# Square sums cast on ScalarE, their columns added by matmuls with ones, and a loader one deeper, in a two-block sequence model on Trainium2

## The chip, the cores and the metric

The kernel runs on one core of one Trainium2 chip. The metric is the device time of one execution in microseconds; several executions of the same kernel are timed and the median is taken. A profile of one execution gives, for every instruction on TensorE (PE, with its weight loads as PEld), VectorE (DVE), ScalarE (ACT), GpSimd (POOL) and SyncE (SP), its start, its duration and what ended the idle time before it.

## The reference, cut to what matters

Two blocks are chained, each on 2048 rows of width 1024, all in float32:

```python
def first_block(x, ...):
    xn = rmsnorm(x, norm_gain)
    proj = xn @ w_in                            # 1024 x 3072
    u, z, h, b, c, zc = pieces of proj, 512 wide each
    y_ssm  = s5_mixer(u, ..., w_glu, b_glu) * silu(z)
             # state-space scan, gelu, then y * sigmoid(y @ w_glu + b_glu)
    y_conv = b * conv3(c * h) * silu(zc)
    return rmsnorm(x + concat(y_ssm, y_conv) @ w_out, final_norm_gain)

def second_block(x, c, ...):
    sh1, sc1, g1, sh2, sc2, g2 = split(silu(c) @ w_ada + b_ada, 6)
    p = (x * (1 + sc1) + sh1) @ w_in_2
    y = concat(conv_module(...),                # 31 taps, layer norm, silu
               hgrn2_mixer(...),                # gated recurrence, 4 heads
               chunk_attention(...)) @ w_out_2  # chunks of 64, 8 chunks back
    x = layer_norm(ALPHA * x + (1 + g1) * y)
    gt, up = split((x * (1 + sc2) + sh2) @ w_ffn_in, 2)    # 2816 each
    return layer_norm(ALPHA * x + (1 + g2) * ((silu(gt) * up) @ w_ffn_out))

reference(x, ...) = second_block(first_block(x, ...), c_2, ...)
```

## The kernel before

Every large product is computed in fp16 with three passes: each float32 operand is scaled by a power of two and split into a high and a low half, and `mm3` (L417, L418, L419) adds high x high, high x low and low x high in one PSUM bank of 128 x 512.

The scale comes from the sum of the operand's squares. The steps, which are those that the change touches, are the same wherever an operand is made ready:

1. `sumsq` (L410): ScalarE squares the tile and leaves one sum for each partition (an ACTIVATE, then an ACTIVATION_READ_ACCUMULATOR of one column). A tile in several pieces has a column for each piece.
2. `part`: VectorE turns the column into bf16 (L365), or adds two columns and writes bf16 (L367). A weight with two or four columns is first added up by a VectorE reduce (L186).
3. `total` (L373): one TensorE matmul with a 128 x 128 matrix of ones adds the column over the partitions and gives every partition the sum. VectorE makes the scale and its inverse out of it (`pow2`, L354 to L356; where the sum itself is kept, a copy to `tot` stands ahead of it).
4. `split`: ScalarE writes the high half (L405), VectorE the low half (L406).

There are 82 such totals. They come from `Weight` (a weight of 128 columns has one column of sums, one of 256 has two, one of 512 has four), `Pair` (an FFN weight, in two pieces: `scale` is the Square and `part`, `cut` the total and the splits), `gp1`/`gp2` and `mp1`/`mp2` (the operands of the GLU and of the first block's out-projection; `mp1` has two columns), and `project` of the FFN, whose column is a VectorE reduce.

A `Loader` takes a list of weights through load (a DMA on SyncE's queue, L169), Square and `part` (`stat`), and total and split (`split`). Each `step` does at most one of each. `d1` is how many loads ahead a Square waits for, `d2` how many loads ahead a split waits for; a weight that is loaded but not split holds its raw float32 tile, 4 KB per partition for 128 columns. `Loader.run` is a generator that other stages advance tick by tick. It passes over a tick when the arena, the pool that all buffers come from, has no room.

The stage around the change of depth is the end of the first block, `stage_glu_mix`. For 16 row blocks t of 128 rows and for each of two halves n of 512 columns it multiplies by `w_out` (24 matmuls), adds the result to x on VectorE (L1079), and calls `k.bg.tick()`, which advances what runs in the background; then come the squares and scale of the final norm, and the tail of the row block before (norm gain, shift, split, the store of x at L1050, two transposing DMAs at L1060). From row block 8 on the background includes `ConvAtt.prep`, whose loader brings in nine weights of the second block's first projections: W0 to W7 with 128 columns, W8 with 256. W0's total stands on TensorE ahead of the second half of row block 9 and W8's ahead of the second half of row block 13. After the sixteen row blocks come the second block's projections from these weights (`proj`).

Each engine runs its instructions in the order in which a scheduler has put them, by its own simulated times, before the program is built. A matmul behind a total in TensorE's order waits with it. `k.several`, `k.pair`, `k.new` and `k.tiny` take buffers from the arena or from a ring of small columns; `k.hold` takes columns that are kept.

Of the kernel before, what the change touches and what calls it, by code (L numbers as in the profile page):

```python
# [11 lines left out]
BF16 = mybir.dt.bfloat16  # L12
# [3 lines left out]
ALU = mybir.AluOpType  # L16
AX = mybir.AxisListType
# [135 lines left out]
class Weight:  # L153
# [17 lines left out]
    def stat(self):  # L171
        k = self.k
        nc = k.nc
        n = len(self.raw)
        self.pair = k.pair([P, self.nkb, self.ncol], "w")
        ss = k.tiny("wss", n)
        for c, raw in enumerate(self.raw):
            if self.colmul is not None:
                cm = self.colmul[:, c * P:(c + 1) * P].unsqueeze(1).to_broadcast([P, self.nkb, P])
                k.gtt(raw, raw, cm, ALU.mult)  # L180
            if self.rowmul is not None:
                self.mul(raw, raw, self.rowmul.unsqueeze(2).to_broadcast([P, self.nkb, P]), ALU.mult)
            k.sumsq(self.pair[1][:, :, c * P:(c + 1) * P].bitcast(BF16), raw, out=ss[:, c:c + 1])
        if n > 1:
            t = k.tiny("wst")
            nc.vector.tensor_reduce(t, ss, axis=AX.X, op=ALU.add)  # L186
            ss = t
        self.cols = k.cols3.pop(0) if len(k.cols3) > 8 else k.hold(3)
        self.tot, self.s, self.inv = (self.cols[:, i:i + 1] for i in range(3))
        self.x = k.part(self.tot, ss)  # L190

    def split(self):
        k = self.k
# [15 lines left out]
class Loader:  # L209
# [6 lines left out]
    def step(self):  # L216
        n, total = self.n, len(self.ws)
        if n[0] < total and n[0] <= n[2] + self.d2:
            self.ws[n[0]].load()
            n[0] += 1  # L220
        if n[1] < n[0] and (n[1] + self.d1 < n[0] or n[0] == total):
            self.ws[n[1]].stat()
            n[1] += 1
        if n[2] < n[1] and (n[2] + self.d2 < n[0] or n[1] == total):
            self.ws[n[2]].split()
            n[2] += 1
        return n[2] < total
# [43 lines left out]
class Kit:  # L271
# [87 lines left out]
    def gtt(self, out, x, y, op):  # L359
        self.nc.gpsimd.tensor_tensor(out, x, y, op)  # L360

    def part(self, col, a, b=None):
        x = col.bitcast(BF16)[:, :1]
        if b is None:
            self.nc.vector.tensor_copy(x, a)  # L365
        else:
            self.nc.vector.tensor_tensor(x, a, b, ALU.add)  # L367
        return x

    def total(self, x, out, tot=None):  # L370
        nc = self.nc
        ps = self.bank()
        nc.tensor.matmul(ps[:, :1], self.ones, x, start=True, stop=True)  # L373
        sq = ps[:, :1]
        if tot is not None:
            nc.vector.tensor_copy(tot, sq)
            sq = tot
        self.pow2(sq, out=out)
        self.unbank(ps)
# [543 lines left out]
def stage_glu_mix(k, a, xT, chunks, ssm, mod, dr, nxt):  # L923
    nc = k.nc
# [49 lines left out]
    def mp1(tb):  # L974
        cv = k.new([P, 4, TB], F32, "cv")
        nc.sync.dma_start(cv, dr["yv"][:, tb * TB:(tb + 1) * TB].rearrange("(k p) t -> p k t", p=P))
        gy = G[tb][0]
        pr = k.pair([P, KB, TB], "mp")
        s2 = k.tiny("ms", 2)
        k.sumsq(pr[1][:, 0:4].bitcast(BF16), gy, out=s2[:, 0:1])  # L980
        k.sumsq(pr[1][:, 4:8].bitcast(BF16), cv, out=s2[:, 1:2])
        s, inv = k.hold(), k.hold()
        k.part(inv, s2[:, 0:1], s2[:, 1:2])
        M[tb] = [gy, cv, pr, s, inv]

    def mp2(tb):
        gy, cv, pr, s, inv = M[tb]
        k.total(inv.bitcast(BF16)[:, :1], (s, inv))
        k.split(pr[0][:, 0:4], pr[1][:, 0:4], gy, s)
        k.split(pr[0][:, 4:8], pr[1][:, 4:8], cv, s)  # L990
        k.free(gy, cv)
        sc = k.hold(2)
        for n in range(2):
            v.tensor_tensor(sc[:, n:n + 1], inv, wo[n].get(0).inv, ALU.mult)
        M[tb] = (pr, sc)

    wl = k.bg.add(wloads(), 1.0)
    for f in range(4):
        w = chunks.get(16 + f, 1)
        for tb in range(NTB):  # L1000
            ps = k.fm(w, xT[tb])
# [19 lines left out]
    gp2(2)  # L1021
    gp1(3)
    mp2(0)
    mp1(1)
    md = dr["mod"][0]
# [6 lines left out]
    g(2)  # L1032
    gp2(3)
    mp2(1)
    xs = {}
    hTs = {}
# [32 lines left out]
    for tb in range(NTB):  # L1069
        pr, sc = M[tb]  # L1070
        for i in range(4):
            t = tb * 4 + i
            if t + 2 < 16:
                load(t + 2)
            x = xs[t]
            for n in range(2):
                ps = k.tm(wo[n].get(0), pr, i)
                xsl = x[:, n * 512:(n + 1) * 512]
                v.scalar_tensor_tensor(xsl, ps, sc[:, n:n + 1], xsl, op0=ALU.mult, op1=ALU.add)  # L1079
                k.unbank(ps)  # L1080
                k.bg.tick()
            junk = k.new([P, D], BF16, "junk")
            ss = k.sumsq(junk, x)
            k.free(junk)
            xs[t] = (x, k.rsqrt(ss, 1.0 / D, 1e-6))
            if t >= 1:
                tail(t - 1)
            if i == 1 and tb + 2 < NTB:
                mp1(tb + 2)
            if i == 3 and tb + 2 < NTB:  # L1090
                mp2(tb + 2)
        k.free(*pr)
        if tb == 0:
            g(3)
        if tb < 3:
            nxt(tb, inv_h, hb2)
# [28 lines left out]
def att_bias(k, a, ext_d, scl):  # L1125
    nc = k.nc
    B = [k.new([P, 640], F32, "B") for _ in range(4)]
    for h in range(4):
        ex = k.new([P, 768], F32, "ex")
        nc.sync.dma_start(ex[:, 511:767], a["rel_bias_2"][0, h, 0:256].partition_broadcast(P))  # L1130
        nc.gpsimd.memset(ex[:, 767:768], 0.0)
        nc.vector.tensor_copy(ex[:, 0:511], ex[:, 511:512].to_broadcast([P, 511]))
        nc.vector.tensor_scalar(ex, ex, scl[h // 2], 8.0, op0=ALU.mult, op1=ALU.mult)
        nc.sync.dma_start(ext_d[h, 0:P * 768].rearrange("(p c) -> p c", p=P), ex)
        k.free(ex)
        yield
    for h in range(4):
        b = B[h]
        nc.sync.dma_start(b, ext_d[h, 127:127 + P * 767].rearrange("(p c) -> p c", p=P)[:, 0:640])
        nc.gpsimd.memset(b[0:64, 576:640], -1e30)  # L1140
        nc.gpsimd.memset(b[64:128, 0:64], -1e30)
        yield
    return B


class ConvAtt:
# [8 lines left out]
    def prep(self, inv_h, hb2):  # L1155
        k, a = self.k, self.a
        nc, v = k.nc, k.nc.vector
        W2 = a["w_in_2"][0]
        W = lambda c0, n=P: Weight(k, W2[:, c0:c0 + n], inv_h, bound=c0 >= 2560)
        self.ws = Loader([W(256), W(384), W(0), W(128), W(2560), W(2816), W(2688), W(2944), W(3072, 256)])  # L1160
        yield from self.ws.run()
        w = self.ws.ws
        self.wg, self.wv, self.wq, self.wk, self.wvv = w[0:2], w[2:4], w[4:8:2], w[5:8:2], w[8]

        def bscale(w):
            q = k.tiny("bq")
            v.tensor_tensor(q, w.tot, hb2, ALU.mult)
            s, i = k.pow2(q, keep=True)
            e = k.hold()
            v.tensor_tensor(e, s, w.inv, ALU.mult)  # L1170
            return s, i, e

        self.sq = [bscale(x) for x in self.wq]
        self.sk = [bscale(x) for x in self.wk]
        self.sv = bscale(self.wvv)
        qks = []
        self.qki = []
        for f in range(2):
            t = k.hold()
            v.tensor_tensor(t, self.sq[f][0], self.sk[f][0], ALU.mult)  # L1180
            qks.append(t)
            t = k.hold()
            v.tensor_tensor(t, self.sq[f][1], self.sk[f][1], ALU.mult)
            v.tensor_scalar(t, t, 0.125, None, op0=ALU.mult)
            self.qki.append(t)
        yield
        self.B = yield from att_bias(k, a, self.dr["ext"], qks)
        self.cw = k.new([P, 2, self.KC], F32, "cw")
        self.cb = k.hold(2)
        for f in range(2):  # L1190
            nc.sync.dma_start(self.cw[:, f], a["conv_w_2"][0][:, f * P:(f + 1) * P].rearrange("j p -> p j"))
        nc.sync.dma_start(self.cb, a["conv_b_2"][0].rearrange("(f p) -> p f", p=P))
        self.gB = k.row(a["conv_ln_g_2"][0], 256)
        self.bB = k.row(a["conv_ln_b_2"][0], 256)
        self.u = k.new([P, 2, 30 + T], F32, "u")
        nc.gpsimd.memset(self.u[:, :, 0:30], 0.0)
# [680 lines left out]
class Pair:  # L1877
# [8 lines left out]

    def scale(self):
        k = self.k
        ss = k.tiny("wss", 3)
        junk = k.new([P, 4, 2 * P], BF16, "junk")  # L1890
        for i in range(2):
            k.sumsq(junk, self.raw[i], out=ss[:, i:i + 1])
        k.free(junk)
        self.inv = k.hold()
        self.x = k.part(self.inv, ss[:, 0:1], ss[:, 1:2])

    def cut(self):
        k = self.k
# [456 lines left out]
```

## Time and profile before

| | |
|---|---|
| median of 3 runs | 3271.31 us (3270.45 to 3274.15) |
| profiled execution: its own time | 3276.22 us |
| profiled execution: span from first to last instruction | 3274.5 us |
| mean granted TensorE clock | 0.967 |
| instructions | 43302 |
| ACT busy, POOL busy | 1116.8 us (34%), 760.0 us (23%) |
| DMA | 364.57 MB, mean 111 GB/s |

A row of the timeline gives the start (us from the span's start), the duration in us, the engine, the line of the kernel, the operation, its output and input by the program's names, the shapes, the count, and in brackets the idle time of that engine before it and what ended that. A row of the groups gives busy time, the mean of one in ns, and the idle time before them. A row of a line's instructions gives the shortest, median and longest duration in ns. A row of the waits gives us in total, times, and the longest. PEclk is the clock that TensorE was granted, as a share of full speed.

### The profile page before, as it was taken

What the parts mean: (1) busy time and instruction counts of PE and PEld (TensorE: products, weight loads), DVE (VectorE), ACT (ScalarE), POOL (GpSimd) and SP (SyncE); (2) the same over time, 40 slices, a digit from 0 to 9 for tenths busy, and PEclk for the clock granted to TensorE, in tenths of its full rate; (3) what the DMA queues carried; (4) which work ended last, traced back from release to release, by engine and by line L of the source; (5) the groups of instructions that cost most, each with busy time, mean ns of one, the idle gap of its engine ahead of it and who ended that gap; (6) DMA issues with size and microseconds to landing.
All of it is one profiled execution on the core that took longest, in us unless ns stands there. A gap on an engine that the chain in (4) does not pass through costs nothing. (4 is left out here: it accounts for less than half of the span.)

```text
span 3274.5 us, 43302 instructions
## 1 busy us (share of the span) xinstructions
PE 3048.2 (93%) x16198; PEld 1532.2 (47%) x16198; DVE 2061.5 (63%) x4895; ACT 1116.8 (34%) x1745; POOL 760.0 (23%) x801
## 2 busy tenths in 40 slices
PE   6799999979799988999999878999999999899998
PEld 4344454534345654555555433444444444344443
DVE  5577887355864469999568877555555555543322
ACT  5322222584524565221333333444443333300000
POOL 0432533023332332110120223111111121023321
PEclk9899999989899998999999989999999999999999
DMA  8734443535773754100125798222331113723220
GB/s 181 166 92 111 121 125 80 120 100 152 215 219 74 138 117 106 39 14 33 62 78 140 170 250 216 90 78 78 102 110 54 58 52 119 244 68 113 68 73 31
DMA packets 549651, 364.57 MB, mean 111 GB/s; under 512 B 290152, under 2 KB 503592, under 8 KB 545344
## 3 DMA queue, kind: packets, MB, share of 16 engines
q1 hardware_dynamic: 549440, 361.81, 41.1%
q8 instruction: 127, 2.08, 0.3%
q14 instruction: 84, 0.69, 0.1%
HBM read 216.73 MB, written 84.70 MB: 92 GB/s over the span
## 5 line engine op out<-in xcount | busy, mean ns | idle before, releaser
L417 PE MATMUL psum<-arena 128*128 128x512 f16 (+2 forms) x4272 | 1601.9, 377 | 78.6 <-DMA arena<-arena 34.4
L418 PE MATMUL psum<-arena 128*128 128x512 f16 (+2 forms) x4272 | 1602.1, 376 | 8.2 <-DMA arena<-h_d 4.2
L419 PE MATMUL psum<-arena 128*128 128x512 f16 (+2 forms) x4272 | 1598.6, 376 | 0.2 <-DVE arena L406 0.2
L360 POOL TENSOR_TENSOR arena<-arena 128x64 f32<-128x64 f32 (+5 forms) x681 | 681.8, 1025 | 2089.2 <-DVE arena L2179 336.9
L417 PEld LDWEIGHTS <-arena 128*128 128x128 f16 x4272 | 426.0, 100 | 593.1 <-issue 101.1
L418 PEld LDWEIGHTS <-arena 128*128 128x128 f16 x4272 | 424.1, 99 | 492.1 <-issue 44.3
L419 PEld LDWEIGHTS <-arena 128*128 128x128 f16 x4272 | 424.2, 99 | 488.4 <-issue 26.1
L410 ACT ACTIVATE arena<-arena 128x1024 bf16<-128x1024 f32 (+2 forms) x218 | 237.7, 1091 | 487.0 <-DVE arena L2062 153.3
L406 DVE SCALAR_TENSOR_TENSOR arena<-arena,kept 128x1024 f16<-128x1024 f32 (+2 forms) x152 | 230.4, 1538 | 130.0 <-ACT arena L405 110.4
L2005 DVE TENSOR_TENSOR arena<-arena,psum 128x512 f32<-128x512 f32 x264 | 177.8, 684 | 206.0 <-PE psum L419 150.9
L405 ACT ACTIVATE arena<-arena,kept 128x1024 f16<-128x1024 f32 (+2 forms) x152 | 174.5, 1175 | 183.0 <-DVE kept L355 62.7
L406 DVE SCALAR_TENSOR_TENSOR arena<-arena,ring 128x1024 f16<-128x1024 f32 (+1 forms) x164 | 209.7, 1302 | 42.0 <-ACT arena L405 36.2
L405 ACT ACTIVATE arena<-arena,ring 128x1024 f16<-128x1024 f32 (+1 forms) x164 | 172.2, 1082 | 168.6 <-DVE ring L355 100.4
L1369 DVE SCALAR_TENSOR_TENSOR arena<-arena 128x512 f32<-128x512 f32 x240 | 177.9, 778 | 0.3
L1551 PE MATMUL psum<-arena 128*127 128x64 f32 (+6 forms) x896 | 106.2, 264 | 22.2 <-DVE arena L1554 21.1
L1551 PEld LDWEIGHTS psum<-arena 128*127 128x127 f32 (+6 forms) x896 | 102.0, 182 | 48.4 <-DVE arena L1554 29.8
L2179 DVE SCALAR_TENSOR_TENSOR arena<-psum,kept,arena 128x512 f32<-128x512 f32 x32 | 23.3, 747 | 144.0 <-PE psum L419 144.0
L770 DVE SCALAR_TENSOR_TENSOR arena<-arena 128x128 f32<-128x128 f32 x336 | 111.6, 367 | 1.8
L2051 ACT ACTIVATE arena<-arena,kept 128x1024 f32<-128x1024 f32 x44 | 49.8, 1142 | 124.1 <-DVE arena L2005 124.1
L1289 ACT ACTIVATE arena<-arena,ring,kept 128x640 f32<-128x640 f32 (+4 forms) x64 | 54.5, 851 | 81.8 <-DVE ring L1287 73.0
L373 PE MATMUL psum<-kept,ones 128*128 128x1 bf16 x82 | 13.3, 169 | 70.4 <-DVE kept L365 49.5
L1553 DVE TENSOR_TENSOR arena<-arena 128x256 f32<-128x256 f32 x112 | 54.9, 490 | 37.4 <-PE psum L1551 35.8
(318 smaller groups left out, 2583.2 us busy)
## 6 DMA issues: line engine op xcount, KB each, us to landing
arena<-in_w_in_dram SPq DMA_DIRECT2D x50, 512.0 KB
arena<-in_w_ada_dram SPq DMA_DIRECT2D x48, 512.0 KB
arena<-in_w_ffn_in_dram SPq DMA_DIRECT2D x44, 512.0 KB
arena<-in_w_ffn_out_dram SPq DMA_DIRECT2D x44, 512.0 KB
a_d<-arena SPq DMA_DIRECT2D x88, 256.0 KB
arena<-a_d SPq DMA_DIRECT2D x40, 512.0 KB
arena<-in_x_dram SPq DMA_DIRECT2D x32, 512.0 KB
x_d<-arena SPq DMA_DIRECT2D x32, 512.0 KB
```

Of the source, the lines that this page charges most:

```text
L360: self.nc.gpsimd.tensor_tensor(out, x, y, op)
L405: self.nc.scalar.activation(hi, src, AF.Identity, scale=s)
L406: self.nc.vector.scalar_tensor_tensor(lo, src, s, hi, op0=ALU.mult, op1=ALU.subtract)
L410: self.nc.scalar.activation(junk, src, AF.Square, accum_out=ss)
L417: self.nc.tensor.matmul(ps, lh, rh, start=start and i == 0, stop=False)
L418: self.nc.tensor.matmul(ps, lh, rl, start=False, stop=False)
L419: self.nc.tensor.matmul(ps, ll, rh, start=False, stop=stop and i == n - 1)
L770: v.scalar_tensor_tensor(ac, raw[:, kb], cc[:, kb:kb + 1], ac, op0=ALU.mult, op1=ALU.add)
L1369: v.scalar_tensor_tensor(acc[:, f], src, w, acc[:, f], op0=ALU.mult, op1=ALU.add)
L1551: nc.tensor.matmul(pv[:rows, bsl], KS[:, c * P:c * P + rows], q4[:, bsl], start=True, stop=True)
L1553: v.tensor_tensor(q4, q4, Fv[:, :, 0:1].to_broadcast([P, nb, hb]), ALU.mult)
L2005: v.tensor_tensor(out, x, ps, op)
```

## The change

Three things are changed:

- `part` is a copy on ScalarE and keeps all columns of sums, up to four, as bf16. VectorE's cast (L365, 56 times), its add (L367, 26 times) and the reduce ahead of it in `Weight.stat` (L186, 7 times) go.
- `total` runs one matmul with ones for each column, all into the same PSUM column, so the columns are added up on TensorE.
- The loader of `ConvAtt.prep` gets `d2=3` instead of 2: a weight's total and split come one tick later, and one more raw tile is held.

```diff
 class Weight: def stat(self):
-        if n > 1:
-            t = k.tiny("wst")
-            nc.vector.tensor_reduce(t, ss, axis=AX.X, op=ALU.add)
-            ss = t
         self.cols = k.cols3.pop(0) if len(k.cols3) > 8 else k.hold(3)
         self.tot, self.s, self.inv = (self.cols[:, i:i + 1] for i in range(3))
-        self.x = k.part(self.tot, ss)
+        self.x = k.part(self.cols[:, 0:2], ss)
...
-    def part(self, col, a, b=None):
-        x = col.bitcast(BF16)[:, :1]
-        if b is None:
-            self.nc.vector.tensor_copy(x, a)
-        else:
-            self.nc.vector.tensor_tensor(x, a, b, ALU.add)
+    def part(self, col, a):
+        x = col.bitcast(BF16)[:, :a.shape[1]]
+        self.nc.scalar.copy(x, a)
         return x

     def total(self, x, out, tot=None):
         nc = self.nc
         ps = self.bank()
-        nc.tensor.matmul(ps[:, :1], self.ones, x, start=True, stop=True)
+        n = x.shape[1]
+        for i in range(n):
+            nc.tensor.matmul(ps[:, :1], self.ones, x[:, i:i + 1], start=i == 0, stop=i == n - 1)
...
 def mp1(tb):
-        k.part(inv, s2[:, 0:1], s2[:, 1:2])
+        k.part(inv, s2)
 def mp2(tb):
-        k.total(inv.bitcast(BF16)[:, :1], (s, inv))
+        k.total(inv.bitcast(BF16)[:, :2], (s, inv))
...
 class ConvAtt: def prep(self, inv_h, hb2):
-        self.ws = Loader([W(256), ..., W(3072, 256)])
+        self.ws = Loader([W(256), ..., W(3072, 256)], d2=3)
...
 class Pair: def scale(self):
-        ss = k.tiny("wss", 3)
+        ss = k.tiny("wss", 2)
-        self.x = k.part(self.inv, ss[:, 0:1], ss[:, 1:2])
+        self.x = k.part(self.inv, ss)
```

More of the change, by code (lines that the diff above doesn't have):

```diff
@@ L1159, in prep @@
         W = lambda c0, n=P: Weight(k, W2[:, c0:c0 + n], inv_h, bound=c0 >= 2560)
-        self.ws = Loader([W(256), W(384), W(0), W(128), W(2560), W(2816), W(2688), W(2944), W(3072, 256)])
+        self.ws = Loader([W(256), W(384), W(0), W(128), W(2560), W(2816), W(2688), W(2944), W(3072, 256)], d2=3)
         yield from self.ws.run()
```

## The prediction

> **What bounds the kernel now.** I read the page first (busy shares, costliest groups), then the waits of TensorE, then the timeline at the long ones, and last the windows around them.
>
> ```profile
> PE 3048.2 (93%) x16198; PEld 1532.2 (47%) x16198; DVE 2061.5 (63%) x4895; ACT 1116.8 (34%) x1745; POOL 760.0 (23%) x801
> L373 PE MATMUL psum<-kept,ones 128*128 128x1 bf16 x82 | 13.3, 169 | 70.4 <-DVE kept L365 49.5
> ...
> PE psum L373 <- DVE kept L365: 49.5, 9, 12.4
> PE psum L373 <- DVE kept L367: 20.2, 3, 18.0
> ```
>
> TensorE is busy for 3048.2 of the span's 3274.5 us, so only its idle time, some 226 us, can be won by moving small work between other engines. The 82 matmuls with ones (L373) stand at the end of 70.4 us of that: in the waits (us in all, times, longest) 49.5 us end with a cast on VectorE (L365), 20.2 with an add (L367). That is the upper bound of the change, and it isn't the forecast, because a wait is put down to the last link of a chain. So the timeline, at three of these waits, all in the stretch where the first block ends and the nine weights W0 to W8 of the second block are made ready:
>
> ```profile
> 843.02 0.19 ACT L410 ACTIVATION_READ_ACCUMULATOR arena<-arena 128x1 f32 x1
> 843.72 2.71 DVE L406 SCALAR_TENSOR_TENSOR arena<-arena,kept 128x1024 f16<-128x1024 f32 x1
> 847.01 0.20 DVE L365 CAST kept<-ring 128x1 bf16<-128x1 f32 x2
> 847.21 0.16 PE L373 MATMUL psum<-kept,ones 128*128 128x1 bf16 x1 [12.37 <-DVE kept L365]
> ...
> 891.07 0.19 ACT L410 ACTIVATION_READ_ACCUMULATOR arena<-arena 128x1 f32 x1
> 891.62 0.15 DVE L365 CAST kept<-ring 128x1 bf16<-128x1 f32 x1
> 891.83 0.16 PE L373 MATMUL psum<-kept,ones 128*128 128x1 bf16 x1 [10.84 <-DVE kept L365]
> ...
> 899.33 1.06 ACT L410 ACTIVATE arena<-arena 128x1024 bf16<-128x1024 f32 x1 [1.13 <-DMA arena<-in_w_in_dram]
> 903.84 0.19 ACT L410 ACTIVATION_READ_ACCUMULATOR arena<-arena 128x1 f32 x1
> 904.36 0.15 DVE L365 CAST kept<-ring 128x1 bf16<-128x1 f32 x1
> 904.56 0.16 PE L373 MATMUL psum<-kept,ones 128*128 128x1 bf16 x1 [5.10 <-DVE kept L365]
> ```
>
> These are the totals of W1, W7 and W8. W1's sum was ready at 843.21 (843.02 + 0.19), but the cast stood behind a 2.71 us split on VectorE and came at 847.01: 3.8 us of queue. W7's sum was ready at 891.26, W8's at 904.03, and their casts began 0.36 and 0.33 us later. There the Square is late, not the cast. Together the three idle times are 28.3 us (12.37 + 10.84 + 5.10). The windows (us long; busy PE, PEld, DVE, ACT, POOL; granted clock; DMA share; GB/s) say who could use them:
>
> ```profile
> 836.00:904.00 68.00, 41.42 (x175) 17.75 (x175) 59.41 (x139) 34.83 (x47) 27.44 (x10) 0.82 0.78 232
> 904.00:962.00 58.00, 57.44 (x291) 29.01 (x291) 48.34 (x89) 19.15 (x25) 26.13 (x36) 0.95 0.81 226
> 962.00:1010.00 48.00, 48.00 (x272) 24.81 (x271) 14.21 (x56) 11.75 (x27) 3.50 (x7) 1.00 0.28 96
> 854.80:860.01 5.21, 5.21 (x27) 2.37 (x25) 3.56 (x6) 2.94 (x3) 2.35 (x1) 1.00 0.72 290
> 904.56:912.50 7.94, 7.94 (x26) 3.01 (x26) 6.77 (x12) 4.45 (x5) 5.63 (x2) 0.65 0.76 297
> ...
> 980.21 0.75 DVE L1254 SCALAR_TENSOR_TENSOR arena<-psum,kept,arena 128x512 f32<-128x512 f32 x1 [14.60 <-PE psum L419]
> ```
>
> From 836 to 904 VectorE is the fullest engine (59.41 of 68 us) and TensorE idles; from 904 to 1010 TensorE has no gap to speak of, and VectorE even waits 14.60 us for it. So what TensorE gains before 904 is kept until 1010, up to about 14.6 us, and no further. The fourth and fifth rows price one half row of the out-projection (24 matmuls): 5.21 us at clock 1.00, 7.94 right after an idle time, at clock 0.65.
>
> **The change, part by part.** The durations and kinds of what goes and comes:
>
> ```profile
> L365 DVE CAST kept<-ring x56: 134/150/158, 9.2 to 2801.0; 128x1 bf16<-128x1 f32 x56
> L367 DVE TENSOR_TENSOR kept<-ring x26: 148/163/1100, 701.0 to 2710.8; 128x1 bf16<-128x1 f32 x26
> L186 DVE TENSOR_REDUCE ring<-ring x7: 143/147/158, 619.7 to 1768.8; 128x1 f32<-128x4 f32 x6, 128x1 f32<-128x2 f32 x1
> 1289.57 0.19 PE L373 MATMUL psum<-kept,ones 128*128 128x1 bf16 x2
> 993.13 0.30 ACT L1291 CAST arena<-arena 128x128 f16<-128x128 f32 x1
> ```
>
> *Removed from VectorE:* 56 x 0.150 + 26 x 0.163 + 7 x 0.147 = 13.7 us over the whole run, spread thinly; about 1 us of it lies in the full stretch. I count it at nothing by itself.
>
> *Deeper loader (W0 to W8).* Load and Square of a weight keep their ticks; only its total and split come one tick later. A tick is one half row of the out-projection (128 rows by 512 columns of a row block), so each total has one half row more of matmuls ahead of it in TensorE's queue. Before, row block 12's second half ended at 880.99 (891.83 - 10.84), W7's total waited to 891.83, row block 13's first half ran, W8's total waited to 904.56, and then came row block 13's second half. After, row block 13's first half stands ahead of W7's total and fills half of that idle time; its second half stands ahead of W8's total, from about 891.6. W8's total still can't come before its Square has ended (904.03) and been cast, say 904.3, and the next thing behind it is now row block 14's first half instead of row block 13's second. TensorE is one half row ahead at 904: 5.2 us by the full-clock row, and 0.25 more since the reduce and cast on VectorE drop out. Bounds from the rows: 0 (the Square moves back by as much) to 14.6. I take 5.4, since W8's Square follows from a DMA and from VectorE's pace, neither of which the loader's depth shortens. The cost of depth is one more raw weight (4 KB per partition) held for a tick; the loader ends one tick later, which is hidden as long as the arena has room.
>
> *W1's cast on ScalarE:* 3.8 us earlier, and one half row runs ahead of it, so most of the 12.37 goes. I count nothing for it: TensorE then runs into the 10.84 before W7, whose Square is set by VectorE at 87% busy. If W1's relief gets through, that is the rival below.
>
> *Other places.* The waits that end with a cast later on, and one in the FFN:
>
> ```profile
> 1281.79 0.18 PE L373 MATMUL psum<-kept,ones 128*128 128x1 bf16 x1 [2.25 <-DVE kept L365]
> 1769.28 0.16 PE L373 MATMUL psum<-kept,ones 128*128 128x1 bf16 x1 [0.72 <-DVE kept L365]
> 1954.11 0.16 PE L373 MATMUL psum<-kept,ones 128*128 128x1 bf16 x1 [18.01 <-DVE kept L367]
> 1977.70 1.10 DVE L367 TENSOR_TENSOR kept<-ring 128x1 bf16<-128x1 f32 x1
> 1978.86 0.16 PE L373 MATMUL psum<-kept,ones 128*128 128x1 bf16 x1 [1.90 <-DVE kept L367]
> 2801.19 0.16 PE L373 MATMUL psum<-kept,ones 128*128 128x1 bf16 x1 [4.02 <-DVE kept L365]
> ```
>
> At 1281.79 some 0.4 of 2.25 us is VectorE's queue; at 1769.28 the reduce and cast go, 0.65 of 0.72; at 1978.86 the add took 1.10 us instead of 0.163, behind other work, and I take 0.5 of the 1.90, half of the 0.94 us by which that add was too long, as the split it releases has its own queue. The 18.01 us at 1954.11 stay: a late Square of the first FFN weight is behind it. Sum: -1.55 us, between 0 and -4.9.
>
> *New cost on ScalarE.* 82 copies of one to four columns. The trace has no such copy on ScalarE; the nearest are the cast of 128 columns, 0.30 us, and the accumulator reads of one column, 0.19 us. So one costs between 0.19 and 0.30; I take 0.22, near the short one, 18 us in all on an engine 34% busy. It is hidden except where ScalarE is full:
>
> ```profile
> 646.00:716.00 70.00, 51.95 (x228) 22.65 (x227) 32.48 (x63) 69.53 (x66) 14.68 (x3) 0.88 0.38 109
> ...
> L405 ACT ACTIVATE arena<-arena,ring 128x1024 f16<-128x1024 f32 (+1 forms) x164 | 172.2, 1082 | 168.6 <-DVE ring L355 100.4
> ...
> 664.30 0.19 ACT L410 ACTIVATION_READ_ACCUMULATOR arena<-arena 128x1 f32 x1
> 664.51 1.28 ACT L945 ACT_TABLE_LOAD   x1
> 665.80 1.08 ACT L945 ACTIVATE arena<-arena 128x512 f32<-128x512 f32 x1
> ```
>
> From 646 to 716 ScalarE is busy 69.53 of 70 us and the GLU stage waits for it; five casts lie there, so 5 x 0.22 = +1.1 us on the path. At 2801 the total's input comes from a VectorE reduce, and a hop to ScalarE replaces the next instruction on the same engine, +0.25, or up to 2.2 if the copy falls behind two of the splits that ScalarE does there (L405, 1.08 us each by the row below). The first total, right after the first cast at 9.2 us, has nothing to hide it: +0.2. Copies that come behind a long Square or split elsewhere: +0.5, from 0 to 2.
>
> *New cost on TensorE.* 26 two-column totals, the two-column W8 and six four-column weights give 26 + 1 + 18 = 45 more matmuls. Two in a row take 0.19 us against 0.16 for one, so 0.03 each: +1.35 us, as TensorE is the path nearly everywhere; 45 x 0.16 = 7.2 would be the other end.
>
> *Sum:* -5.4 - 1.55 + 1.1 + 0.25 + 0.2 + 0.5 + 1.35 = -3.55 us against the profiled execution, which took 3276.2 us for a span of 3274.5. The median of the runs is 3271.3, 4.9 lower, so I take the difference to it: 3267.7. A measurement of this kernel tells about 0.2%, 6.5 us, from no change; 3267.7 is a gain inside that.
>
> **The rivals.**
>
> *More relief.* W1's 12.37 and W7's 10.84 both shrink, because rows that start earlier let VectorE work ahead. For it: VectorE has 8.6 us idle in 836 to 904, and much of it follows W1's late start. Against: it is 87% busy there, and W7's Square follows from it. The bound is the 14.60 us that VectorE waits for TensorE at 980: -14.6 - 1.55 + 3.4 = -12.75, 3258.6.
>
> *Nothing.* The half row won is lost again, to a wait for a PSUM bank or for VectorE, which lags: +1.85 with the small terms, 3273.2 at most, and 3271 if these are smaller than I have them.
>
> *Slower: W8's load a round later.* The place is between 865 and 904.
>
> ```profile
> 884.68 0.34 SPq L1050 DMA_DIRECT2D x_d<-arena  x1
> 892.03 2.36 SPq L169 DMA_DIRECT2D arena<-in_w_in_dram  x2
> 898.31 0.34 SPq L1050 DMA_DIRECT2D x_d<-arena  x1
> ```
>
> W8's two loads stand on SyncE behind one row block's store and ahead of the next; the stores follow each other every 13.6 us (898.31 - 884.68). They landed at about 899.3, where the Square row quoted above was released by them. If the raw weight held one tick longer leaves no buffer for W8, its load slips behind the next store, by 13.6 us. The total then comes at 904.3 + 13.6 = 917.9 with row block 14's first half behind it, which started at 912.50 before: 5.4 us lost instead of won, -1.55 + 3.4 + 5.4 = +7.25, 3278.6. It decides from 5.4 us of delay of that Square (no gain there) and costs over 0.2% from about 13.
>
> *Slower: table loads.* In 646 to 716 the scheduler mixes Squares with gelu, sigmoid and silu, and a switch costs 1.28 us, with the next ACTIVATE 0.01 us after the load. Five casts more on ScalarE can change that order. By rows, three extra switches (3.8 us) eat the forecast gain, eight (10.2 us) make it slower by 0.2%: 3278. The Trainium skill, "ScalarE: Activation LUTs", section "What ACT_TABLE_LOAD costs", puts a drain of 1380 ns beside the 1283 ns of the load, 2.66 us a switch, by which four switches would do; the rows at 664 have the load but no room for such a drain. The same page, section "Table sets: the hidden batching unit", has copy in every set, so a cast alone would ask for no switch; no run here shows one of these copies yet. The order alone could do it, and the chance is small.
>
> **How the numbers follow.** My forecast 0.45, with a range of its own from 3263 to 3272; about a third of it (0.14) lies below 3264.8, the limit of 0.2%. More relief 0.27, all of it faster. Nothing 0.08. The late load 0.12 and the table order 0.08, both slower. Faster 0.27 + 0.14 = 0.41, the same 0.31 + 0.08 = 0.39, slower 0.20. The range runs from 3254 (more relief, with the small terms at their good ends) to 3280 (either slower case): outside it I leave about 0.1 on each side.
>
> **What would show it.** In the trace after: no cast, add or reduce of columns on VectorE (L186, L365, L367), 82 copies on ScalarE near 0.2 us each, 127 matmuls with ones; in W1 to W8, one half row more ahead of each total; idle before W1's total under 4 us, before W7's still 4 to 6 (a half row of 5.2 less), before W8's about 5; VectorE's wait for TensorE near 980 shorter by 5 us. ScalarE's full stretch at 646 to 716 longer by about 1 us, with no table load more. Wrong would be: W7's idle time gone as well (more relief), W8's loads after a later store, more table loads, or the same idle time moved to the totals' next readers.

## The result and the profile after

The changed kernel takes 3291.55 us (median of 4 runs, 3285.99 to 3294.62) against 3270.88 for the kernel before in the same sessions: a ratio of 1.0066, interval 1.005 to 1.0082, so some 21 us slower where 3.6 us faster was forecast, and above the forecast range, which ended at 3280. Three executions among all the runs of this document took 5.4 to 14.1 ms; the ratios leave them out, so a ratio need not be the quotient of the two medians beside it. The changed kernel's profiled execution took 3285.99 us, its fastest run, while that of the kernel before (3276.22) lies above all its runs there; a second profile of the kernel before took 3269.53 (span 3267.8). So the two first traces, 9.8 us apart in span, show about half of the difference.

The page after:

```profile
span 3284.3 us, 43397 instructions
PE 3056.4 (93%) x16243; PEld 1542.5 (47%) x16243; DVE 2059.0 (63%) x4806; ACT 1122.1 (34%) x1823; POOL 757.7 (23%) x801
```

The casts on ScalarE (L360) and the matmuls with ones (now L368), each line's instructions with the shortest, median and longest duration in ns:

```profile
L360 ACT CAST kept<-ring x82: 175/193/198, 10.2 to 2810.9; 128x1 bf16<-128x1 f32 x49, 128x2 bf16<-128x2 f32 x27, 128x4 bf16<-128x4 f32 x6
L368 PE MATMUL psum<-kept,ones x127: 163/167/211, 10.5 to 2811.2; 128*128 128x1 bf16 x127
```

Four of these matmuls in a row on the timeline, the total of a 512-wide weight:

```profile
1280.89 0.24 PE L368 MATMUL psum<-kept,ones 128*128 128x1 bf16 x4
```

And TensorE's waits that end at them:

```profile
PE psum L368 <- ACT kept L360: 32.2, 7, 10.9
PE psum L368 <- DVE arena L401: 13.4, 1, 13.4
```

The change does what it says: 82 casts on ScalarE, 127 matmuls with ones, and the idle time of TensorE in front of these falls from 70 to 46 us. In the stretch of W0 to W8 it worked, too, as the timeline after shows:

```profile
841.94 0.16 PE L368 MATMUL psum<-kept,ones 128*128 128x1 bf16 x1 [3.64 <-ACT kept L360]
858.58 0.59 PE L412 MATMUL psum<-arena 128*128 128x512 f16 x1 [3.45 <-DVE arena L1074]
...
873.12 0.38 PE L412 MATMUL psum<-arena 128*128 128x512 f16 x1 [1.15 <-DVE arena L1074]
...
879.32 0.38 PE L412 MATMUL psum<-arena 128*128 128x512 f16 x1 [0.86 <-DVE arena L1074]
...
884.50 0.17 PE L368 MATMUL psum<-kept,ones 128*128 128x1 bf16 x1
...
886.36 0.38 PE L412 MATMUL psum<-arena 128*128 128x512 f16 x1 [1.69 <-DVE arena L1074]
...
902.36 0.18 ACT L360 CAST kept<-ring 128x2 bf16<-128x2 f32 x1
902.59 0.19 PE L368 MATMUL psum<-kept,ones 128*128 128x1 bf16 x2 [10.89 <-ACT kept L360]
```

and its windows:

```profile
836.00:904.00 68.00, 46.32 (x192) 19.72 (x191) 53.95 (x114) 34.36 (x53) 26.52 (x10) 0.83 0.77 218
904.00:962.00 58.00, 58.00 (x315) 30.79 (x314) 47.93 (x98) 19.52 (x25) 23.80 (x26) 0.99 0.76 219
```

W1's wait is 3.64 us instead of 12.37, W7's total (884.50) comes without any, W8's waits 10.89 instead of 5.10: 14.5 us at these three totals instead of 28.3. Of the 13.8 us saved, 7.2 come back as waits for VectorE's add to x (L1074), behind the totals of W3, W5, W6 and W7, where the kernel before has none. TensorE is busy 46.32 us from 836 to 904, 4.9 more than before, and has no idle time at all from there to 962. Where the time goes shows in the first and last start of two lines, the attention's score matmuls (L1280 before, L1275 after) and the recurrence's (L1551, L1546). Before:

```profile
L1280 PE MATMUL psum<-arena x280: 216/219/314, 990.3 to 1262.4; 128*128 128x128 f16 x140
L1551 PE MATMUL psum<-arena x896: 219/268/471, 1302.7 to 1830.2; 128*127 128x64 f32 x28, 128*120 128x64 f32 x27, 128*96 128x64 f32 x27, 128*126 128x64 f32 x25
```

and after:

```profile
L1275 PE MATMUL psum<-arena x280: 216/219/314, 981.8 to 1261.2; 128*128 128x128 f16 x140
L1546 PE MATMUL psum<-arena x896: 219/268/476, 1301.6 to 1846.5; 128*127 128x64 f32 x27, 128*120 128x64 f32 x27, 128*96 128x64 f32 x27, 128*126 128x64 f32 x25
```

The attention starts 8.5 us earlier, ends 1.2 earlier, and the recurrence ends 16.3 us later: the attention has grown from 272.1 to 279.4 us, the recurrence from 527.5 to 544.9. Neither holds much that was changed. Later the wait for the first FFN weight is 13.44 us after, against 18.01 in the first profile of before and 16.1 in the second, so 3 to 5 us come back there.

### The profile page after: what moved, and what is told of

It is laid out like the page before. It is cut to its first block, busy times and chain, and to the rows that moved or that the text cites. A ratio compares the mean times of both kernels' runs of the same rounds, so it can differ in the third digit from the quotient of the medians.

```text
span 3284.3 us, 43397 instructions
## 1 busy us (share of the span) xinstructions
PE 3056.4 (93%) x16243; PEld 1542.5 (47%) x16243; DVE 2059.0 (63%) x4806; ACT 1122.1 (34%) x1823; POOL 757.7 (23%) x801
## 4 chain that ended last, share of the span: by engine, by line
PE 46%; DVE 6%; DMA 2%; issue 1%; POOL 1%; ACT 1%; SPq 0%; DVEq 0%; POOLq 0%; ACTq 0%
PE psum L414 14%; PE psum L413 14%; PE psum L412 14%; PE psum L1546 2%; DVE arena L1364 1%; DVE arena L401 1%; POOL arena L356 1%; DMA arena<-arena 0%; DVE arena L1549 0%; ACT arena L400 0%; DVE arena L1548 0%; DVE arena L1765 0%; PE psum L1583 0%; DMA arena<-in_ln_b_dram 0%; PE psum L1588 0%
## 5 line engine op out<-in xcount | busy, mean ns | idle before, releaser
L414 PEld LDWEIGHTS <-arena 128*128 128x128 f16 x4272 | 424.3, 99 | 490.1 <-issue 28.3
L401 DVE SCALAR_TENSOR_TENSOR arena<-arena,ring 128x1024 f16<-128x1024 f32 (+1 forms) x164 | 201.6, 1274 | 14.9 <-ACT arena L400 14.4
L1546 PE MATMUL psum<-arena 128*127 128x64 f32 (+6 forms) x896 | 109.7, 270 | 27.6 <-DVE arena L1549 23.1
L1546 PEld LDWEIGHTS psum<-arena 128*127 128x127 f32 (+6 forms) x896 | 105.6, 188 | 54.6 <-DVE arena L1549 32.7
L2181 DVE SCALAR_TENSOR_TENSOR arena<-arena,kept 128x1024 f32<-128x1024 f32 x16 | 22.2, 1386 | 83.3 <-DMA arena<-x_d 83.3
```

The source lines that it names most:

```text
L401: self.nc.vector.scalar_tensor_tensor(lo, src, s, hi, op0=ALU.mult, op1=ALU.subtract)
L414: self.nc.tensor.matmul(ps, ll, rh, start=False, stop=stop and i == n - 1)
L1546: nc.tensor.matmul(pv[:rows, bsl], KS[:, c * P:c * P + rows], q4[:, bsl], start=True, stop=True)
```

## The experiments

### Which part of the change

Three parts, each alone or left out. Depth alone (the kernel before with one argument more):

```diff
-        self.ws = Loader([W(256), ..., W(3072, 256)])
+        self.ws = Loader([W(256), ..., W(3072, 256)], d2=3)
```

> The kernel before with the loader of W0 to W8 one deeper (d2=3) and nothing else; casts and adds stay on VectorE, one matmul with ones per total. Theory 'depth' (the loss of the second block comes from the loader ending a tick later, which shifts what the scheduler puts where behind it): TensorE 5 to 9 us earlier at the second block's first projections, then lost, 8 to 20 us slower at the end, ratio 1.003 to 1.006. Theory 'cast' (the loss comes from the casts on ScalarE): the 5 to 9 us are kept, 3262 to 3267, ratio 0.997 to 0.9985. Theory 'columns' (the loss comes from the added matmuls): as 'cast'.

The whole change with the depth put back to 2:

> The changed kernel with the loader's depth put back (d2=2); casts on ScalarE and a matmul with ones per column stay. 'Depth': within 3 us of before, less the small terms of the prediction (ratio 0.999 to 1.001). 'Cast': slower by 15 to 28 us (ratio 1.005 to 1.008), the loss again between 1200 and 1830 us. 'Columns': as 'cast'.

Columns added by matmuls, cast on VectorE, depth 2:

```diff
-        self.nc.scalar.copy(x, a)
+        self.nc.vector.tensor_copy(x, a)
```

> Columns kept and added by matmuls with ones, but cast on VectorE, depth 2. 'Columns': slower by 15 to 28 us. 'Cast' and 'depth': within 3 us of before (45 matmuls of 0.03 us more, 33 VectorE instructions of 0.15 us fewer).

The kernel before, only the single-column casts on ScalarE:

```diff
         if b is None:
-            self.nc.vector.tensor_copy(x, a)
+            self.nc.scalar.copy(x, a)
```

> The kernel before with only the 56 single-column casts moved to ScalarE; the 26 adds of two columns and the 7 reduces stay on VectorE, one matmul per total, depth 2. 'Cast': slower by 10 to 28 us. 'Depth' and 'columns': within 3 us of before. If all four are off by different amounts in the second block without a common part, then it is the order that the scheduler writes that differs from kernel to kernel, and none of the three parts has a price of its own there.

| kernel | median, us | before, us | ratio and interval |
|---|---|---|---|
| depth alone | 3280.95 | 3265.06 | 1.0053 (1.0039 to 1.0066) |
| casts and columns, depth 2 | 3268.94 | 3265.06 | 1.0012 (1.0003 to 1.002) |
| columns, cast on VectorE, depth 2 | 3270.48 | 3265.06 | 1.0016 (1.0007 to 1.0025) |
| single casts on ScalarE, depth 2 | 3271.99 | 3265.06 | 1.0017 (1.0008 to 1.0026) |

The depth is what costs: 16 of some 21 us. The three others cost 4 to 7 us each: more than the 3 us that theory 'depth' allowed them, and far less than the 10 us and more of the other two theories. They don't add up (all casts and columns cost no more than either part), and the kernel before, run a second time against itself, came out 3 us apart (next table), so no single price can be read from them.

### Why the depth costs: where the tiles lie

Two theories were left. "Early arrival": TensorE comes earlier to a stretch that VectorE bounds, and gains nothing. "Layout": the raw tile held one tick longer moves what is allocated after it. When the program's construction is followed step by step, the second says more: with depth 3 the kept tiles of W8 and others lie elsewhere in the arena, and so the 512-wide weights of the recurrence, whose halves need 8 KB per partition in one piece each, find room at other moments. The first of them is refused eight times instead of ten and is squared at tick 48 instead of 50 (ticks counted from the start of the attention's stage), the recurrence starts at tick 49 instead of 50, and the second is loaded at tick 50 instead of 52. Everything behind is written in another order. The arena was therefore given a list of places:

```diff
-    def take(self, n):
+    def take(self, n, pin=-1):
...
+        for run in runs:
+            if pin >= run[0][0] and pin + n <= run[-1][1]:
+                best = (None, pin)
```

With it, depth 3 can run with the places of depth 2 and the other way round; from the attention on, the program has the same allocations in the same order as the kernel whose places it takes. The three kernels above with depth 2 have the allocations of the kernel before throughout, and so are runs on the old places too. The kernel before was also run again, for a second profile.

> The kernel before, unchanged, for a second profile of it: its first profiled execution was 3276.2 us where the median of 26 runs is 3265. Both theories: 3261 to 3268, with the difference to the first profile at waits for DMA and at a higher granted clock, not in the order of instructions.

> Depth 3 alone, with every tile of the arena from the loader on put at the address that it has in the kernel before (two tiles that would collide lie elsewhere for a while), so that the second block's program is written in exactly the order of before; only the nine weights' totals are a tick later. Theory 'layout' (the deeper loader leaves W0 to W8 at other addresses, the 512-wide weight of the recurrence finds room two ticks earlier, and the program from there on has another order, which costs VectorE time): TensorE 8 to 9 us earlier at the attention and still 5 to 9 at the end, 3256 to 3261, ratio 0.997 to 0.9985. Theory 'early arrival' (TensorE's gain is lost since VectorE, the bound from 1200 us on, isn't any earlier, and the depth itself costs): 3265 to 3281, ratio 1.000 to 1.005.

> Depth 2 as before, but the tiles at the addresses that they have with depth 3, so that the second block's program is written in exactly the order of the run with depth 3 alone. 'Layout': no gain at 975 us and the whole loss behind it, slower than depth 3 alone: 3284 to 3294, ratio 1.006 to 1.009. 'Early arrival': as before, 3262 to 3268, ratio 0.999 to 1.001.

> The whole change (casts on ScalarE, columns by matmuls, depth 3) with the tiles at the addresses of before. 'Layout': as depth 3 with the old layout, plus the 4 us that casts and columns cost at depth 2: 3259 to 3266, ratio 0.998 to 1.0005. 'Early arrival': 3280 to 3292, ratio 1.004 to 1.008.

| kernel | median, us | before, us | ratio and interval |
|---|---|---|---|
| before, again | 3270.26 | 3267.27 | 1.0006 (0.9991 to 1.0021) |
| depth 3, old places | 3264.86 | 3267.27 | 0.9994 (0.998 to 1.0009) |
| depth 2, new places | 3284.09 | 3267.27 | 1.0057 (1.0042 to 1.0071) |
| whole change, old places | 3265.84 | 3267.27 | 0.9991 (0.9978 to 1.0003) |

The places alone, without any part of the change, cost 17 us. The depth without them shows no cost (0.9994, interval 0.998 to 1.0009). The first and last starts for depth 3 with old places (its lines are 100 further down):

```profile
L1380 PE MATMUL psum<-arena x280: 216/219/311, 986.5 to 1258.1; 128*128 128x128 f16 x140
L1651 PE MATMUL psum<-arena x896: 219/268/469, 1298.0 to 1824.8; 128*127 128x64 f32 x28, 128*120 128x64 f32 x27, 128*96 128x64 f32 x27, 128*126 128x64 f32 x25
```

for depth 2 with new places (lines likewise 100 further down):

```profile
L1380 PE MATMUL psum<-arena x280: 216/219/314, 986.2 to 1264.7; 128*128 128x128 f16 x140
L1651 PE MATMUL psum<-arena x896: 219/268/475, 1303.8 to 1845.7; 128*127 128x64 f32 x27, 128*120 128x64 f32 x27, 128*96 128x64 f32 x27, 128*126 128x64 f32 x25
```

and for depth alone:

```profile
L1280 PE MATMUL psum<-arena x280: 216/219/314, 981.1 to 1263.5; 128*128 128x128 f16 x140
L1551 PE MATMUL psum<-arena x896: 219/268/475, 1301.8 to 1837.8; 128*127 128x64 f32 x27, 128*120 128x64 f32 x27, 128*96 128x64 f32 x27, 128*126 128x64 f32 x25
```

With the old places the attention takes 271.6 us and the recurrence 526.8, as in the two profiles of the kernel before (272.1 and 527.5; 271.5 and 526.7). With the new places it is 278.5 and 541.9 at depth 2, 282.4 and 536.0 at depth 3. Over all profiles so far the two groups don't overlap: the seven kernels with the old places lie at 269.8 to 272.1 and 520.4 to 527.5 us, the three with the new ones at 278.5 to 282.4 and 536.0 to 544.9. "Early arrival" falls: depth 3 with old places starts the attention 3.8 us earlier and ends the recurrence 5.4 us earlier than the first profile of before (3.7 and 3.9 us earlier than the second). The early start itself, expected to be 8 to 9 us with the old places, is half depth and half places: 3.8 us and 4.1 us alone, 9.2 together.

Most of the attention's loss stands in one wait, 7.47 us long, and shortly ahead of it the second 512-wide weight is loaded by four DMAs on SyncE's queue. Before:

```profile
1234.75 4.75 SPq L169 DMA_DIRECT2D arena<-in_w_in_dram  x4
```

and after, with a wait of TensorE's behind them:

```profile
1200.39 0.53 SPq L169 DMA_DIRECT2D arena<-in_w_in_dram  x1
1201.66 1.67 SPq L169 DMA_DIRECT2D arena<-in_w_in_dram  x2
1213.31 0.49 SPq L169 DMA_DIRECT2D arena<-in_w_in_dram  x1
...
1222.71 0.27 PE L1275 MATMUL psum<-arena 128*128 128x128 f16 x1 [7.47 <-DVE ring L1279]
```

They run 34 us earlier, among the attention's transposing DMAs, and TensorE then waits 7.47 us for a softmax of VectorE's at 1222.71. That the earlier load causes this wait is not shown. In the stretch from the middle of the attention to three quarters of the recurrence, TensorE's waits (us in total, times, longest) show where more of it is. In the second profile of before:

```profile
PE psum L1551 <- DVE arena L1554: 16.6, 12, 2.6
PE psum L1280 <- DVE ring L1284: 1.9, 2, 1.5
```

and with depth alone:

```profile
PE psum L1551 <- DVE arena L1554: 22.0, 13, 3.7
PE psum L1280 <- DVE ring L1284: 8.8, 5, 6.3
PE psum L1588 <- ACT arena L1604: 3.0, 2, 2.6
```

### Which step of the new order costs

> Depth 3 alone with its own layout, but the Square of the first 512-wide weight of the recurrence is refused ten times, as many times as it found no room in the kernel before. Theory 'room' (it is that this weight finds room two ticks earlier from which the other order follows): the loss shrinks from 16 us to 0 to 6, 3262 to 3272, and the waits for the attention's transposing DMAs near 1200 us go. Theory 'addresses' (the new places of the tiles themselves make instructions wait for each other, whatever the order): still 3278 to 3286, ratio 1.004 to 1.0065.

```diff
 class Weight: def stat(self):
+        if self.late > 0:
+            self.late -= 1
+            raise MemoryError
...
+        wi.late = 10
```

3281.35 us against 3269.84, ratio 1.0031 (1.0019 to 1.0043). The first and last starts (the scores' line is 4 further down here, the recurrence's 5):

```profile
L1284 PE MATMUL psum<-arena x280: 216/219/314, 985.5 to 1263.4; 128*128 128x128 f16 x140
L1556 PE MATMUL psum<-arena x896: 219/268/469, 1305.9 to 1831.4; 128*120 128x64 f32 x27, 128*96 128x64 f32 x27, 128*64 128x64 f32 x27, 128*127 128x64 f32 x25
```

The recurrence is back at 525.5 us, the attention, at 277.9, isn't. So "room" is half right: in this profile, which lies 5 us below its kernel's median, holding the weight back removes the recurrence's loss, and by the ratios (1.0053 alone, 1.0031 here, whose intervals just overlap) it removes some two fifths of the cost. But it doesn't bring the old order back: the recurrence now starts two ticks earlier than in the kernel before, since the tiles that it waited for found room in front of that weight.

> Depth 3 alone with its own layout, and the rate at which the convolution's taps (240 VectorE operations of 0.75 us) are mixed into the recurrence lowered from 2.8 to 2.5. Theory 'taps' (the 9 us lost in the first quarter of the recurrence are the 15 taps more that stand there, 15 x 0.75 = 11 us of VectorE, the fullest engine): 5 to 9 us faster than depth 3 alone, 3270 to 3277, with about 150 taps by the end of that quarter. Theory 'chain' (the quarter is slow for its waits, and fewer taps don't help): 3278 to 3290.

3286.44 us against 3269.84, ratio 1.0051 (1.0036 to 1.0066): no faster than depth alone. The taps are spread out further and end 83 us later. With depth alone:

```profile
L1369 DVE SCALAR_TENSOR_TENSOR arena<-arena x240: 710/743/1894, 1212.6 to 1558.0; 128x512 f32<-128x512 f32 x120
```

and with the lower rate:

```profile
L1369 DVE SCALAR_TENSOR_TENSOR arena<-arena x240: 720/743/1887, 1215.2 to 1641.4; 128x512 f32<-128x512 f32 x120
```

The recurrence takes 539.8 us (1303.8 to 1843.6) instead of 536.0. The first quarter of the recurrence as a window, with depth alone:

```profile
1302.00:1442.00 140.00, 129.84 (x753) 76.54 (x753) 135.43 (x343) 31.90 (x86) 19.41 (x11) 0.98 0.08 27
```

and with the lower rate:

```profile
1304.00:1446.00 142.00, 132.39 (x760) 78.84 (x759) 110.80 (x300) 35.48 (x89) 17.58 (x10) 0.96 0.08 27
```

"Taps" falls: there VectorE has 25 us less to do at the lower rate, and the quarter is as long. VectorE's load isn't what lengthens the recurrence there. That leaves the other theory, the chain of waits from engine to engine, which no run shows by itself.

One more run was to tell whether the second 512-wide weight's load, among the attention's DMAs, costs the attention its 7 us: depth 3 with this load put off by three refusals, expected 6 to 9 us faster than depth alone if so. It gave no result, since the arena runs out of room later in that program, and so this cause stays open.

### Other places, nothing else

If places alone decide, any shift of them should. The arena prefers places that were freed at least 24 frees ago to younger ones; this constant alone was changed.

```diff
-        self.sb = Arena(..., n, 8, 24, small=264, zone=44032)
+        self.sb = Arena(..., n, 8, 25, small=264, zone=44032)
```

> The kernel before (depth 2, casts and adds on VectorE) with one constant of the arena changed, the age up to which a freed place is passed over: 25 frees instead of 24. Nothing of the change is in it; its tiles lie elsewhere, and in its program the first 512-wide weight of the recurrence gets its Square at tick 47 instead of 50 and the recurrence starts at tick 48. Theory 'layout' (the second block's time hangs on the places and the order that follows, whatever moved them): slower, 3273 to 3290, ratio 1.002 to 1.007, the loss between 1130 and 1830 us. Theory 'depth' (the loss has to do with the loader): 3263 to 3270, ratio 0.999 to 1.0015.

> As the one before, with 26: the 512-wide weight gets its Square at tick 46, and the recurrence starts only at tick 57, seven later than in the kernel before. 'Layout': slower, 3275 to 3300, ratio 1.003 to 1.01. 'Depth': 3263 to 3270.

25 gives 3307.13 us against 3268.3, ratio 1.0118 (1.0103 to 1.0133); 26 gives 3315.47, ratio 1.0145 (1.0127 to 1.0163). Both are further than expected. With 25:

```profile
L1280 PE MATMUL psum<-arena x280: 216/219/311, 992.1 to 1271.1; 128*128 128x128 f16 x140
L1551 PE MATMUL psum<-arena x896: 219/268/473, 1314.4 to 1858.3; 128*96 128x64 f32 x28, 128*127 128x64 f32 x26, 128*126 128x64 f32 x26, 128*120 128x64 f32 x26
```

279.0 and 543.9 us: the same two stretches, by nearly the same amounts as after the change, 23 us of the 32 by which this profile is longer than the first one of before; the rest lies around them. With 26 the order is another one:

```profile
L1280 PE MATMUL psum<-arena x280: 216/219/314, 994.9 to 1234.6; 128*128 128x128 f16 x140
L1551 PE MATMUL psum<-arena x896: 219/268/472, 1320.4 to 1867.0; 128*127 128x64 f32 x28, 128*120 128x64 f32 x27, 128*96 128x64 f32 x26, 128*126 128x64 f32 x25
```

The attention takes only 239.7 us, but the recurrence starts 17.7 us later than before and takes 546.6, so it ends 36.8 us later. The loss is not bound to the order that the change brought. Of all the sets of places that were run, those of the kernel before are the fastest; these two and those of the change cost 0.5% to 1.5%.

## Why the prediction was wrong, point by point

**The step that failed** is in the part on the deeper loader: "The cost of depth is one more raw weight (4 KB per partition) held for a tick; the loader ends one tick later, which is hidden as long as the arena has room." Room there was: no buffer was refused to this loader. But the tile moved others, and the sum puts the cost of that at nothing without a reason. Depth 2 with the new places measured it: 17 us (1.0057), more than four times the whole forecast gain. The sum ended at 1010 us, where TensorE's lead was 8.5 us; nothing in it looked at what the second block would do with other places.

**The rivals.** "W8's load a round later" named the arena as the danger, and held 0.12 of the chance for it, but with the wrong mechanism: W8's Square wasn't late. Its total ran at 902.59, 2 us earlier than before. "More relief" came true where it was looked for, with 8.5 us at the attention's start where I had 5.4, and was of no use at the end. VectorE's wait for TensorE near 980, its bound, is 3.16 us where it was 14.60 and where 5 us less was forecast: 8.5 us of the difference are TensorE's lead, 2.9 are VectorE, which starts to wait at 968.52 where it started at 965.61.

```profile
971.68 0.75 DVE L1249 SCALAR_TENSOR_TENSOR arena<-psum,kept,arena 128x512 f32<-128x512 f32 x1 [3.16 <-PE psum L414]
```

"Nothing" came in part, by the mechanism that it named: the waits for VectorE's add (L1074) are 3.45, 1.15, 0.86 and 1.69 us, half of what the totals of W1, W7 and W8 no longer wait. The table loads were wrong: the stretch from 646 to 716 has 15 of them after the change and 16 before, and the six casts in it take 1.1 us, as the sum had it.

**The gain at W0 to W8**, forecast as 5.4 us, was 3.8 for depth with the old places (986.5 against 990.3), and 8.5 in the changed kernel, where the places added some of their own. That the size comes near the forecast is in part luck, since the idle times behind it did not come as forecast. The mechanism (one half row more ahead of each total) is seen in W7's total. That W7's wait would still be 4 to 6 us and W8's 5 was wrong: W7's is gone and W8's is 10.89.

**The whole change without its side effect**, on the old places, is 0.9991 (0.9978 to 1.0003) of before, which is 2.9 us faster, with an interval that takes in the 3.6 us forecast and no change as well. So the sum of the direct terms is not contradicted, but an interval as wide as that confirms none of them.

**Small terms.** A cast on ScalarE takes 0.193 us, 0.22 was taken. Four matmuls with ones take 0.24 us and one 0.16, 0.027 for each more, 0.03 was taken. At 2811.17 the wait is 4.76 instead of 4.02, 0.74 more where 0.25 was taken. The Trainium skill, "ScalarE: Activation LUTs", section "What ACT_TABLE_LOAD costs", gives an ACTIVATE with immediate scale and bias 186 ns and 0.833 ns for each element, an estimated 0.187 us for one column. The trace lists these copies as an instruction of another kind, CAST, for which that figure isn't given; at 0.193 us they come close to it.

**What stays open.** The runs with given places fix the order of the program and the places together. Whether the 17 us come from the order of instructions or from tiles that must wait for the ones whose place they take was not separated; the held-back weight suggests that the recurrence's part follows from when that weight is made ready. Why the three parts at depth 2 cost 4 to 7 us while the whole change on the old places costs nothing beside depth 3 alone (0.9991 against 0.9994) wasn't settled either. Places are not the reason, since these three have the allocations of before; the intervals leave room for 4 us.

## What to carry to other kernels

Where a kernel places its own buffers, holding one buffer longer is a change to every allocation behind it: before costing such an edit by its own stage, list the allocations and refusals of the stages that follow, and see whether the order of the program changes there. To measure an edit by itself, hand the allocator the old places; and to know how much of a tuned time is luck of places, change one constant of the allocator and nothing else (here 39 and 47 us). Here a gain read from one stage was kept only where the stages behind it had the old allocations.

## What the runs showed that was not expected

A lead of TensorE was not lost although VectorE is the fullest engine behind it: with unchanged places the 3.8 us at the attention's start were still there at the recurrence's end (5.4 us against the first profile of before, 3.9 against the second). In the whole time they are not clear of the noise (0.9994). And an engine that was busy nearly all the time of a stretch was not its bound: VectorE in the first quarter of the recurrence, as the two windows above show.
